# Scaling the first two blocks of x before their transposes, with the front's matmuls in a fixed order

## The chip, the cores and the metric

One core of one Trainium2 chip runs the kernel. The metric is the device time of one execution in microseconds (us), as a median over executions. For this kernel, a difference under 0.5% (3.6 us) is about what a measurement can't tell from no change.

## What is computed

One decoder layer on x of 512 tokens by 2048 features, in float32. What matters here is its start:

```python
c_act = jax.nn.silu(c)
mod = c_act @ w_ada + b_ada
shift, scale, gate = jnp.split(mod, 3, axis=-1)
h = rms_norm(x) * (1.0 + scale) + shift      # rms_norm: x * rsqrt(mean(x*x over features) + EPS)
proj = h @ w_in                              # 2048 -> 4160 columns
# then an RG-LRU branch, an attention branch, an output projection, x + gate * y
```

## The kernel before

Everything after the start works on x transposed: a block k is 128 features (partitions) by 512 tokens, and there are 16 blocks. The input projection `h @ w_in` runs over chunks of 2, 3, 4 and 7 blocks; its first chunk needs blocks 0 and 1 alone. TensorE (PE) works through its instructions in the order that a scheduler fixed when the kernel was built, and so do VectorE (DVE) and ScalarE (ACT). All loads of this part are issued by SyncE (SP) in the written order.

The front, up to the first projection matmul, does this:

- `xsq` loads x token-major in eight pieces `xtok` (128 tokens by 1024 features). ACT squares each and adds up per token. Of the four pieces that hold features 0 to 255, PE transposes two 128x128 tiles each into the PSUM banks `xps[0]` and `xps[1]`. These become blocks 0 and 1 of x.
- `warm(n)` issues n matmuls on a constant tile (`junk`), whose result nobody reads; they keep TensorE busy while it would have nothing to do.
- DVE and ACT turn the sums into the factor `rx` (one number per token, on partitions). Four PE matmuls (`rb_ps`) turn it into a row that is repeated on all partitions, and block 0 is multiplied by it.
- The scale of block 0, `mod[:, 16]`, is made by 16 PE matmuls with one output column each (`m_ps<-ccol,m`), eight from each of two loaded tiles `m0`. All other columns of `mod` are made by DVE: `ttr`, L277, multiplies a row block of the transposed w_ada (`ada`) with silu(c) and sums. `ada(j, parts)` does this for column j in several loads; the parts count in units of 512.
- `make_h(0)` computes `xs` = x block 0 * scale + shift on DVE. `proj_first` multiplies it in full float32 with the first weights (`pp<-xs,wfraw`, 8 matmuls, each of which shows as two rows in the trace), and then block 1, split into a high part `hh[1]` and a low part `hl[1]` (`pp<-h,wfs`, 24 matmuls). `make_h(1)` first needs four more pieces of `ada` (columns 17 and 1). From there on PE goes through weight groups (`pp<-h,whi` and `wlo`) without another kind of matmul for a long time.

Of the kernel before, what the change touches and what calls it, by code (L numbers as in the profile page):

```python
# [12 lines left out]
F32 = mybir.dt.float32  # L13
# [3 lines left out]
AF = mybir.ActivationFunctionType  # L17
ALU = mybir.AluOpType
AX = mybir.AxisListType

P = 128
S = 512
D = 2048
NK = D // P
NT = S // P
# [13 lines left out]
XSTEPS = (36, 40)  # L39
P0 = 8  # L40
SETUP = (0, 2)
WARM = (4, 6, 4, 2, 6)
NACC = 6
GRATE = 1.1
BANKS = dict(u=(0, 1), f=(2,), sc=(4, 5), tp=(6,), op=(6,), tq=(7,), oa=(2, 3, 0, 1, 7, 4, 5, 6))
# [37 lines left out]
def body(ctx, nc, tc, a):  # L83
    V, G, A, PE, DMA = nc.vector, nc.gpsimd, nc.scalar, nc.tensor, nc.sync
    last_tab = [None]

    def act(out, in_, func, **kw):
        return A.activation(out=out, in_=in_, func=func, **kw)  # L88

    def tab(out, in_, func, **kw):  # L90
        if last_tab[0] is None:
            i = act(out, in_, func, **kw)
        else:
            with tc.issue_after(last_tab[0]):
                i = act(out, in_, func, **kw)
        last_tab[0] = i.ins if hasattr(i, "ins") else i
        return i

    def stt(out, in0, scalar, in1, op0, op1, **kw):
        return V.scalar_tensor_tensor(out=out, in0=in0, scalar=scalar, in1=in1, op0=op0, op1=op1, **kw)  # L100
# [3 lines left out]
    def behind():  # L104
        return tc.issue_after(mark[0]) if mark[0] is not None else nullcontext()

    def ins_of(i):
        return i.ins if hasattr(i, "ins") else i

    def ts(o, i, s1, s2, o0, o1=None):  # L110
        if s2 is None:
            return V.tensor_scalar(out=o, in0=i, scalar1=s1, scalar2=None, op0=o0)
        return V.tensor_scalar(out=o, in0=i, scalar1=s1, scalar2=s2, op0=o0, op1=o1)

    def tt(o, x, y, op):
        return V.tensor_tensor(out=o, in0=x, in1=y, op=op)  # L116

    def split(hi, lo, src):
        act(hi, src, AF.Copy)
        return tt(lo, src, hi.bitcast(F32), ALU.subtract)  # L120

    def mm(out, lhsT, rhs, start, stop, **kw):
        return PE.matmul(out=out, lhsT=lhsT, rhs=rhs, start=start, stop=stop, **kw)  # L123
# [6 lines left out]
    def cols(i):  # L130
        return slice(i * P, (i + 1) * P)
# [14 lines left out]
    def run(gen):  # L146
        for _ in gen:
            pass
# [18 lines left out]
    def bank(kind, name):  # L167
        return psp.tile([P, S], F32, tag=f"b{next(cyc[kind])}", name=name)
# [3 lines left out]
    def pjt(n, dt=F32, name=None):  # L172
        return pj.tile([P, S], dt, tag=f"pj{n}", name=name or f"pj{n}")

    def bigt(n, name, dt=F32):
        return big.tile([P, 2, S], dt, tag=f"B{n}", name=name)
# [26 lines left out]
    ident = row[:, R_ID:R_ID + P]  # L203
# [16 lines left out]
    ccol = p1.tile([P, NK], F32, name="ccol")  # L220
# [23 lines left out]
    def warm(n, after=None):  # L244
        with tc.issue_after(ins_of(after)) if after is not None else nullcontext():
            for _ in range(n):
                mm(junk_ps, junk[:, :P], junk, True, True)

    warm(WARM[0])
    cps = [bank("mm", "cb_ps") for _ in range(4)]  # L250
# [9 lines left out]
    xt = {}  # L260
# [14 lines left out]
    def ttr(t, cv, j, first, last):  # L275
        with behind():
            ttr_last[0] = V.tensor_tensor_reduce(  # L277
                out=t, in0=t, in1=cv, op0=ALU.mult, op1=ALU.add, scale=1.0,
                scalar=vec[:, C_BADA + j:C_BADA + j + 1] if first else modh[:, j:j + 1],
                accum_out=(mod if last else modh)[:, j:j + 1])  # L280

    def ada(j, parts=(4,)):
        t = p1.tile([P, 4, S], F32, tag="ada", name="ada", bufs=3)
        n0 = 0
        for w in parts:
            c = slice(n0, n0 + w)
            DMA.dma_start(out=t[:, c], in_=a["ada"][j][:, n0 * S:(n0 + w) * S].rearrange("p (k s) -> p k s", k=w))
            ttr(t[:, c], cb[:, c], j, n0 == 0, n0 + w == 4)
            n0 += w
            yield  # L290
# [79 lines left out]
    def xsq(i, j):  # L370
        t = bigt((2, 3, 8, 9, 10, 11, 12, 13)[2 * i + j], "xtok").rearrange("p k s -> p (k s)")
        DMA.dma_start(out=t, in_=a["xtok"][i][:, j * 1024:(j + 1) * 1024])
        sq = act(sqj, t, AF.Square, accum_out=ss8[:, j * 4 + i:j * 4 + i + 1])
        if j == 0:
            for k in range(KT0):
                PE.transpose(xps[k][:, i * P:(i + 1) * P], t[:, k * P:(k + 1) * P], ident)
        warm(WARM[1], sq)

    hh, hl = {}, {}
    KT0 = CHUNKS[0][1]  # L380
    NG = NF // 4
    wfs = {(k, n): bigt(4 + k * NG + n, "wfs", F32R) for k in range(1, KT0) for n in range(NG)}
# [12 lines left out]
    xps = [bank("mm", "xps") for k in range(KT0)]  # L395
    for n in range(2 * NT):
        xsq(n // 2, n % 2)
# [3 lines left out]
    m0 = [bigt(4 + q, "m0").rearrange("p k s -> p (k s)").rearrange("p (b f) -> p b f", b=8) for q in range(2)]  # L401
    for q in range(2):
        DMA.dma_start(out=m0[q], in_=a["ada0"][:, 8 * q:8 * q + 8])
    run(ada(0, (2, 1, 1)))
    for n in range(NG):
        wf_load(0, n)
    tab(p1.tile([P, 1], F32, name="sqrt0"), ones[:, 0:1], AF.Sqrt)
    for k in range(KT0):
        xt[k] = pjt(34 + k, F32, f"x{k}")
        act(xt[k], xps[k], AF.Copy)  # L410


    vx, yx, tx, rx = (p1.tile([P, NT], F32, name=n) for n in ("vx", "yx", "tx", "rx"))
    tt(vx, ss8[:, 0:4], ss8[:, 4:8], ALU.add)
    ts(vx, vx, 1.0 / D, EPS, ALU.mult, ALU.add)
    warm(WARM[2], V.reciprocal(out=tx, in_=vx))
    tab(yx, tx, AF.Sqrt)
    tt(tx, yx, yx, ALU.mult)
    stt(tx, tx, -0.5, vx, ALU.mult, ALU.mult)
    mark[0] = ins_of(stt(rx, tx, 1.5, yx, ALU.add, ALU.mult))  # L420
    rb_ps = bank("aux", "rb_ps")
    for i in range(NT):
        mm(rb_ps[:, cols(i)], rx[:, i:i + 1].broadcast_to([P, P]), ident, True, True)
    rb = p1.tile([P, S], F32, tag="rb", name="rb")
    tt(xt[0], xt[0], rb_ps, ALU.mult)
    act(rb, rb_ps, AF.Copy)
    m0_ps = bank("mm", "m0_ps")
    for b in range(NK):
        i = mm(m0_ps[:, 0:1], m0[b // 8][:, b % 8], ccol[:, b:b + 1], b == 0, b == NK - 1)
        if b % 8 == 7:  # L430
            warm(WARM[3] if b < NK - 1 else WARM[4], i)
    tt(mod[:, 16:17], m0_ps[:, 0:1], vec[:, 16:17], ALU.add)

    h0 = []
# [1 line left out]
    def make_h(k):  # L436
        if 0 < k < KT0:
            yield from ada(16 + k, (2, 2))
            yield from ada(k, (2, 2))
        x, sc, sh = xt[k], mod[:, 16 + k:17 + k], mod[:, k:k + 1]  # L440
        t = bigt(k, f"h{k}", F32R)
        hh[k], hl[k] = t[:, 0], t[:, 1]
        if k < KT0:
            xs = pjt(30 + k, F32, "xs")
            if k == 0:
                h0.append(xs)
                mark[0] = ins_of(ts(xs, x, sc, sh, ALU.mult, ALU.add))
                split(hh[k], hl[k], xs)
                for k1 in range(1, KT0):
                    with behind():  # L450
                        tt(xt[k1], xt[k1], rb, ALU.mult)
            else:
                act(xs, x, AF.Copy, scale=sc)
                ts(hh[k], xs, sh, None, ALU.add)
                mark[0] = ins_of(stt(hl[k], xs, sh, hh[k].bitcast(F32), ALU.add, ALU.subtract))
        else:
            stt(x, x, sc, rb, ALU.mult, ALU.mult)
            act(hh[k], x, AF.Identity, bias=sh)
            stt(hl[k], x, sh, hh[k].bitcast(F32), ALU.add, ALU.subtract)
        if not k:  # L460
            yield
# [14 lines left out]
    def row_sums(n):  # L476
        while summed[0] < n:
            row_load()
            mark[0] = wlast[0]
            j = rows[summed[0]]  # L480
            ttr(tiles.pop(0), cb, j, True, True)
            summed[0] += 1
            if j < 16:
                run(make_h(j))

    run(make_h(0))
    run(make_h(1))
    for n in range(NG):
        wf_load(1, n)
# [238 lines left out]
    for n, m in enumerate(MORDER[:24]):  # L728
# [23 lines left out]
        for n0, t0 in ((7, 0), (15, 4)):  # L752
            if n0 <= n < n0 + 4:
                t = t0 + n - n0
# [474 lines left out]
```

## Time and profile before

| | us |
|---|---|
| median of 3 timed runs | 726.15 (726.0, 726.15, 728.82) |
| profiled execution, its own time | 725.46 |
| its span, first to last instruction | 723.7 |

The rows below come from the profiled execution; times in them count from the start of its span. A row of the timeline has the start and the duration of one instruction, or of several of a kind that follow each other, with their number (x16). In brackets stand the idle time of the engine before it and what ended that. A matmul's duration is modelled and runs past the start of the next, so that the distance between starts tells what it costs. PEld is TensorE's weight load, which goes on beside the matmul before it.

### The profile page before, as it was taken

How to read it: one execution, taken by the hardware profiler on the slowest of the kernel's cores; microseconds unless marked ns; L12 is line 12 of the kernel's file. 1: busy time of each engine (PE TensorE's matmuls, PEld its weight loads, DVE VectorE, ACT ScalarE, POOL GpSimd, SP SyncE). 2: the span in 40 equal slices, each digit the busy share in tenths (PEclk: the TensorE clock that was granted, in tenths of full speed). 3: DMA queues.
4: the chain of work that ended last, by engine and by line, in shares of the span. 5: the costliest groups of instructions: out<-in, count | busy, mean ns of one | idle time of the engine just before them, and what ended most of it. 6: DMA issues, size and time to landing. Idle time of an engine off the chain costs nothing.

```text
span 723.7 us, 10053 instructions
## 1 busy us (share of the span) xinstructions
PE 718.7 (99%) x3608; PEld 596.0 (82%) x3608; DVE 525.6 (73%) x945; ACT 354.2 (49%) x729; POOL 29.4 (4%) x34
## 2 busy tenths in 40 slices
PE   9999999999999999999999999999999999999998
PEld 4688888888888888888898898898888887888886
DVE  2867999998998889888755566567686786683232
ACT  7277222222233589884455578587465534222221
POOL 0000000000000000001011011111020100000000
PEclk9999999999999999999999999999999999999999
DMA  8998777877613321232342225213334685974330
GB/s 303 408 401 317 297 275 270 352 262 271 241 36 101 108 89 69 90 102 77 93 140 95 81 77 186 71 47 132 125 124 141 219 290 191 318 264 171 115 95 29
DMA packets 46145, 127.95 MB, mean 177 GB/s; under 512 B 5516, under 2 KB 9484, under 8 KB 42512
## 3 DMA queue, kind: packets, MB, share of 16 engines
q1 hardware_dynamic: 39040, 106.35, 41.3%
q10 hardware_dynamic: 7056, 20.97, 8.3%
q8 instruction: 28, 0.46, 0.3%
q14 instruction: 21, 0.17, 0.1%
HBM read 123.11 MB, written 4.19 MB: 176 GB/s over the span
## 4 chain that ended last, share of the span: by engine, by line
PE 99%; DVE 0%; ACT 0%; issue 0%
PE pp L123 48%; PE oa L123 24%; PE sc L123 4%; PE uwuv L123 3%; PE uwqn L123 3%; PE uwuk L123 3%; PE op L123 2%; PE junk_ps L123 2%; PE uqp L123 2%; PE tp L926 1%; PE pk L123 1%; PE tq L826 1%; PE pi L123 1%; PE pr L123 1%; PE tqe L881 0%; PE m_ps L123 0%
## 5 line engine op out<-in xcount | busy, mean ns | idle before, releaser
L123 PE MATMUL pp<-h,whi 128*128 128x512 f32 x992 | 241.1, 390 | 0.0
L88 ACT ACTIVATE whi<-wraw 128x512 fp32r<-128x512 f32 (+4 forms) x172 | 127.0, 741 | 227.7 <-PE pp L123 98.9
L123 PEld LDWEIGHTS pp<-h,whi 128*128 128x128 f32 x992 | 185.1, 188 | 38.3 <-issue 0.4
L116 DVE TENSOR_TENSOR wlo<-wraw,whi 128x512 fp32r<-128x512 f32 (+4 forms) x172 | 141.4, 824 | 72.0 <-ACT whi L88 33.9
L123 PE MATMUL pp<-h,wlo 128*128 128x512 f32 x496 | 126.7, 390 | 0.0
L123 PEld LDWEIGHTS pp<-h,wlo 128*128 128x128 f32 x496 | 92.9, 188 | 19.2
L123 PE MATMUL oa<-yh,whi 128*128 128x512 f32 (+1 forms) x260 | 100.9, 393 | 0.1
L123 PE MATMUL oa<-yl,whi 128*128 128x512 f32 (+1 forms) x260 | 101.0, 389 | 0.0
L116 DVE TENSOR_TENSOR pj<-pp,pj 128x512 f32<-128x512 f32 x96 | 65.0, 689 | 16.6 <-PE pp L123 15.9
L123 PE MATMUL oa<-yh,wlo 128*128 128x512 f32 (+1 forms) x260 | 71.2, 390 | 0.0
L277 DVE CUSTOM_DVE_ANT_0 ada<-ada,cb,vec 128x2048 f32<-128x2048 f32 (+1 forms) x31 | 69.6, 2247 | 1.5 <-DMA ada<-in_ada 1.5
L123 PEld LDWEIGHTS oa<-yl,whi 128*128 128x128 f32 x260 | 49.0, 188 | 9.3 <-DVE yl L116 0.2
L123 PEld LDWEIGHTS oa<-yh,whi 128*128 128x128 f32 x260 | 48.9, 188 | 9.4 <-ACT yh L88 0.3
L123 PEld LDWEIGHTS oa<-yh,wlo 128*128 128x128 f32 x260 | 48.0, 188 | 9.5
L123 PE MATMUL sc<-kT,qT 128*128 128x128 f32 (+3 forms) x96 | 22.5, 331 | 0.0
L918 DVE TENSOR_REDUCE nm<-sc 128x1 f32<-128x128 f32 (+3 forms) x32 | 15.5, 487 | 8.0 <-PE sc L123 7.9
L229 POOL TENSOR_TENSOR hs<-hs,mhalf 128x8 f32<-128x8 f32 x12 | 21.2, 1768 | 1.0
L88 ACT ACTIVATE pr<-sc,nm 128x128 f32<-128x128 f32 (+3 forms) x32 | 16.7, 522 | 9.1 <-DVE nm L918 9.0
L123 PE MATMUL uwuv<-whi,kvt 128*128 128x256 f32 x80 | 20.8, 284 | 0.0
L123 PE MATMUL uwqn<-whi,kvt 128*128 128x256 f32 x80 | 20.7, 286 | 0.0
L277 DVE CUSTOM_DVE_ANT_0 ada<-ada,cbo,modh 128x1024 f32<-128x1024 f32 x16 | 20.5, 1281 | 0.0
L277 DVE CUSTOM_DVE_ANT_0 ada<-ada,cbo,vec 128x1024 f32<-128x1024 f32 x16 | 20.5, 1280 | 0.0
(234 smaller groups left out, 995.8 us busy)
## 6 DMA issues: line engine op xcount, KB each, us to landing
ada<-in_ada SPq DMA_DIRECT2D x28, 1024.0 KB, 7.0
ada<-in_ada ACTq DMA_DIRECT2D x32, 512.0 KB, 5.1
wraw<-in_wout SPq DMA_DIRECT2D x59, 256.0 KB, 3.6
wraw<-in_win SPq DMA_DIRECT2D x22, 512.0 KB, 6.2
wraw<-in_win SPq DMA_DIRECT2D x24, 448.0 KB, 3.2
wraw<-in_win SPq DMA_DIRECT2D x16, 384.0 KB, 5.6
xtok<-in_xtok SPq DMA_DIRECT2D x8, 512.0 KB, 6.6
xo<-in_x SPq DMA_DIRECT2D x16, 256.0 KB, 5.0
```

Source lines behind the costliest of these rows:

```text
L88: return A.activation(out=out, in_=in_, func=func, **kw)
L116: return V.tensor_tensor(out=o, in0=x, in1=y, op=op)
L123: return PE.matmul(out=out, lhsT=lhsT, rhs=rhs, start=start, stop=stop, **kw)
L229: G.tensor_tensor(out=out, in0=out, in1=mhalf[:, :n], op=ALU.pow)
L277: ttr_last[0] = V.tensor_tensor_reduce(out=t, in0=t, in1=cv, op0=ALU.mult, op1=ALU.add, scale=1.0, scalar=vec[:, C_BADA + j:C_BADA + j + 1 ...
L826: PE.transpose(tp[:, d * 256 + i2 * P:d * 256 + (i2 + 1) * P], kt[u][:, q * P:(q + 1) * P], ident)
L918: V.tensor_reduce(out=nm, in_=sp[:, :n], axis=AX.X, op=ALU.max, negate=True)
L926: PE.transpose(tp[:, j * P:(j + 1) * P], pr[:, j * P:(j + 1) * P], ident)
```

## The change

The four head pieces of `xtok` (256 features each) are multiplied by `rx` in place, two on DVE and two on ACT, while still token-major. Then they are transposed, so that the blocks in PSUM are already normalized. Block 0 stays in PSUM and `xs` reads it there; block 1 is copied by ACT. The matmuls of the front get a fixed order: eight `m_ps`, four `rb_ps`, two warm ones, eight transposes, eight `m_ps`, three warm ones. `ada(0)` comes in two parts instead of three. The warm matmuls go from 4 + 48 + 4 + 2 + 6 = 64 to 4 + 42 + 2 + 3 = 51.

```diff
-WARM = (4, 6, 4, 2, 6)
+WARM = (4, 6, 2, 3)
...
         if j == 0:
-            for k in range(KT0):
-                PE.transpose(xps[k][:, i * P:(i + 1) * P], t[:, k * P:(k + 1) * P], ident)
-        warm(WARM[1], sq)
+            xhead.append(t[:, :KT0 * P])
+        if 2 * i + j < 2 * NT - 1:
+            warm(WARM[1], sq)
...
-    run(ada(0, (2, 1, 1)))
+    run(ada(0, (2, 2)))
...
-    for k in range(KT0):
-        xt[k] = pjt(34 + k, F32, f"x{k}")
-        act(xt[k], xps[k], AF.Copy)
...
-    warm(WARM[2], V.reciprocal(out=tx, in_=vx))
+    V.reciprocal(out=tx, in_=vx)
...
+    m0_ps = bank("mm", "m0_ps")
+    for i in range(NT):
+        if i % 2:
+            ts(xhead[i], xhead[i], rx[:, i:i + 1], None, ALU.mult)
+        else:
+            act(xhead[i], xhead[i], AF.Copy, scale=rx[:, i:i + 1])
+    for b in range(NK // 2):
+        i = mm(m0_ps[:, 0:1], m0[0][:, b], ccol[:, b:b + 1], b == 0, False)
     rb_ps = bank("aux", "rb_ps")
-    for i in range(NT):
-        mm(rb_ps[:, cols(i)], rx[:, i:i + 1].broadcast_to([P, P]), ident, True, True)
+    with tc.issue_after(ins_of(i)):
+        for i in range(NT):
+            t = mm(rb_ps[:, cols(i)], rx[:, i:i + 1].broadcast_to([P, P]), ident, True, True)
+    warm(WARM[2], t)
+    with tc.issue_after(ins_of(t)):
+        for i in range(NT):
+            for k in range(KT0):
+                t = PE.transpose(xps[k][:, cols(i)], xhead[i][:, cols(k)], ident)
+    with tc.issue_after(ins_of(t)):
+        for b in range(NK // 2):
+            i = mm(m0_ps[:, 0:1], m0[1][:, b], ccol[:, NK // 2 + b:NK // 2 + b + 1], False, b == NK // 2 - 1)
+    xt[0] = xps[0]
+    for k in range(1, KT0):
+        xt[k] = pjt(34 + k, F32, f"x{k}")
+        act(xt[k], xps[k], AF.Copy)
+    warm(WARM[3], i)
     rb = p1.tile([P, S], F32, tag="rb", name="rb")
-    tt(xt[0], xt[0], rb_ps, ALU.mult)
     act(rb, rb_ps, AF.Copy)
-    m0_ps = bank("mm", "m0_ps")
-    for b in range(NK):
-        i = mm(m0_ps[:, 0:1], m0[b // 8][:, b % 8], ccol[:, b:b + 1], b == 0, b == NK - 1)
-        if b % 8 == 7:
-            warm(WARM[3] if b < NK - 1 else WARM[4], i)
...
                 split(hh[k], hl[k], xs)
-                for k1 in range(1, KT0):
-                    with behind():
-                        tt(xt[k1], xt[k1], rb, ALU.mult)
```

On TensorE, the part between the factor and the scale of block 0 stood like this before (`m_ps` is the scale of block 0, `rb_ps` the repeated factor; the second warm pair is left out):

```order
L123 MATMUL m_ps<-ccol,m_230 128x1 x7
L123 MATMUL rb_ps<-row,rx 128x128 x4
L123 MATMUL m_ps<-ccol,m_230 128x1
L123 LDWEIGHTS junk
L123 MATMUL junk_ps<-junk 128x512
...
L123 MATMUL m_ps<-ccol,m_231 128x1 x8
```

With the change, the same part of TensorE's order is this:

```order
L123 MATMUL m_ps<-ccol,m_216 128x1 x8
L123 MATMUL rb_ps<-row,rx 128x128 x4
L123 LDWEIGHTS junk
L123 MATMUL junk_ps<-junk 128x512
...
L435 MATMUL xps<-row,xtok 128x128 x8
L123 MATMUL m_ps<-ccol,m_217 128x1 x8
```

The eight transposes (`xps`), which stood among the warm matmuls ahead of this part, now stand between the two halves of `m_ps`. Ahead of this part, 23 warm matmuls follow directly behind the `cb_ps` matmuls.

On VectorE, from the first piece of `ada(0)` to `xs` of block 0, the difference is this (ISA is the multiply-and-sum of `ttr` and its read-out):

```order
 L277 ISA ada,modh<-ada,cb,vec 128x1024
 L277 ISA modh 128x1
-L277 ISA ada,modh<-ada,cb,modh 128x512
-L277 ISA modh 128x1
-L116 TENSOR_TENSOR x_245<-x_245,rb_ps 128x512
-L277 ISA ada,mod<-ada,cb,modh 128x512
+L277 ISA ada,mod<-ada,cb,modh 128x1024
 L277 ISA mod 128x1
 L116 TENSOR_TENSOR mod<-m_ps,vec 128x1
-L113 TENSOR_SCALAR xs<-x_245,mod 128x512
-L116 TENSOR_TENSOR x_247<-x_247,rb 128x512
+L113 TENSOR_SCALAR xs<-xps,mod 128x512
```

Both products with the repeated factor are gone, two half pieces of `ada(0)` have become one, and `xs` reads PSUM. The two products on head pieces of `xtok` stand ahead of the first row.

## Rows read from the trace of the kernel before

**Rows 1.** From the profile's page: busy time of each engine, and the share of the span by engine in the chain of work that ended last.

```profile
PE 718.7 (99%) x3608; PEld 596.0 (82%) x3608; DVE 525.6 (73%) x945; ACT 354.2 (49%) x729; POOL 29.4 (4%) x34
...
PE 99%; DVE 0%; ACT 0%; issue 0%
```

**Rows 2.** Timeline of TensorE's matmuls, from the end of `cb_ps` to the first weight group.

```profile
10.28 1.07 PE L123 MATMUL cb_ps<-c4l,sel 4*128 4x512 f32 x4
...
15.01 2.97 PE L123 MATMUL junk_ps<-junk 128*128 128x512 bf16 x13
17.82 0.38 PE L376 MATMUL xps<-row,xtok 128*128 128x128 f32 x2
18.04 1.46 PE L123 MATMUL junk_ps<-junk 128*128 128x512 bf16 x6
19.33 1.62 PE L123 MATMUL m_ps<-ccol,m 128*128 128x1 f32 x14
20.81 1.14 PE L123 MATMUL rb_ps<-row,rx 128*128 128x128 f32 x8
21.79 0.28 PE L123 MATMUL m_ps<-ccol,m 128*128 128x1 f32 x2
21.93 0.59 PE L123 MATMUL junk_ps<-junk 128*128 128x512 bf16 x2
22.36 1.84 PE L123 MATMUL m_ps<-ccol,m 128*128 128x1 f32 x16
24.06 1.46 PE L123 MATMUL junk_ps<-junk 128*128 128x512 bf16 x6
25.35 7.03 PE L123 MATMUL pp<-xs,wfraw 128*128 128x512 f32 x16
31.87 6.00 PE L123 MATMUL pp<-h,wfs 128*128 128x512 f32 x24
37.70 1.07 PE L123 MATMUL pp<-h,whi 128*128 128x512 f32 x4
```

**Rows 3.** Timeline of VectorE, from its copy of `cb` to the high part of block 1.

```profile
10.69 1.29 DVE L258 COPY cb<-cb_ps 128x512 f32<-128x512 f32 x2 [4.72 <-PE cb_ps L123]
...
18.59 0.16 DVE L100 SCALAR_TENSOR_TENSOR rx<-tx,yx 128x4 f32<-128x4 f32 x1
20.02 1.28 DVE L277 CUSTOM_DVE_ANT_0 ada<-ada,cb,vec 128x1024 f32<-128x1024 f32 x1 [1.26 <-DMA ada<-in_ada]
...
22.06 0.69 DVE L116 TENSOR_TENSOR x<-x,rb_ps 128x512 f32<-128x512 f32 x1
...
24.24 0.16 DVE L116 TENSOR_TENSOR mod<-m_ps,vec 128x1 f32<-128x1 f32 x1 [0.82 <-PE m_ps L123]
24.43 0.55 DVE L113 TENSOR_SCALAR xs<-x,mod 128x512 f32<-128x512 f32 x1
24.89 0.69 DVE L116 TENSOR_TENSOR x<-x,rb 128x512 f32<-128x512 f32 x1
25.50 1.28 DVE L277 CUSTOM_DVE_ANT_0 ada<-ada,cb,vec 128x1024 f32<-128x1024 f32 x1
...
29.84 1.28 DVE L277 CUSTOM_DVE_ANT_0 ada<-ada,cb,modh 128x1024 f32<-128x1024 f32 x1
...
31.24 0.49 DVE L112 TENSOR_SCALAR h<-xs,mod 128x512 fp32r<-128x512 f32 x1
31.76 0.75 DVE L100 SCALAR_TENSOR_TENSOR h<-xs,mod,h 128x512 fp32r<-128x512 f32 x1
```

**Rows 4.** Timeline of ScalarE: the first product with a factor per partition, and the high parts of block 1's weights.

```profile
28.63 0.72 ACT L88 ACTIVATE xs<-x,mod 128x512 f32<-128x512 f32 x1 [2.98 <-DVE mod L277]
29.95 1.31 ACT L88 ACTIVATE wfs<-wfraw 128x512 fp32r<-128x512 f32 x2 [0.60 <-DMA wfraw<-in_winf]
```

**Rows 5.** Answers by tile. First the matmuls on the first weights (number of rows; duration in ns, shortest/median/longest; first and last start). Then loads, each with its issue and, in the line below, the time to its landing: the first `m0` tile, the third piece of `ada(0)`, and the four pieces of `ada` for columns 17 and 1.

```profile
L123 PE MATMUL pp<-xs,wfraw x16: 592/592/592, 25.4 to 31.8; 128*128 128x512 f32 x16
...
L403 SPq DMA_DIRECT2D m<-in_ada x1: 327/327/327, 7.6 to 7.6; - x1
...
DMA to landing us min/median/max: 9.8/9.8/9.8
...
L287 SPq DMA_DIRECT2D ada<-in_ada x1: 328/328/328, 13.4 to 13.4; - x1
...
DMA to landing us min/median/max: 7.9/7.9/7.9
...
L287 SPq DMA_DIRECT2D ada<-in_ada x4: 327/328/431, 16.4 to 20.0; - x4
...
DMA to landing us min/median/max: 9.0/9.2/9.3
```

**Rows 6.** Stretches of the span: busy time of the engines (with the number of instructions), the granted TensorE clock, the DMA share and GB/s.

```profile
20.00:24.00 4.00, 4.00 (x37) 3.85 (x37) 3.36 (x7) 0.60 (x1) 0.00 (x0) 1.00 1.05 396
24.00:28.00 4.00, 4.00 (x15) 1.95 (x16) 3.73 (x7) 0.63 (x1) 0.00 (x0) 1.00 1.03 404
```

**Rows 7.** The same of the warm matmuls alone, in two stretches (PE busy with its number of instructions, clock, DMA share, GB/s).

```profile
1.60:6.60 5.00, 5.00 (x12) 1.00 0.68 203
12.30:14.70 2.40, 2.40 (x12) 1.00 1.02 414
```

**Rows 8.** Timeline of VectorE at the turn from the first chunk to the second.

```profile
71.51 0.96 DVE L116 TENSOR_TENSOR wlo<-wraw,whi 128x768 fp32r<-128x768 f32 x1 [4.39 <-ACT pj L88]
```

More of the change, by code (lines that the diff above doesn't have):

```diff
@@ L374, in xsq @@
         if j == 0:
-            for k in range(KT0):
-                PE.transpose(xps[k][:, i * P:(i + 1) * P], t[:, k * P:(k + 1) * P], ident)
-        warm(WARM[1], sq)
-    hh, hl = {}, {}
+            xhead.append(t[:, :KT0 * P])
+        if 2 * i + j < 2 * NT - 1:
+            warm(WARM[1], sq)
+    hh, hl, xhead = {}, {}, []
     KT0 = CHUNKS[0][1]
```

## The prediction

> **What bounds the kernel now.** I read the page first. TensorE is busy 99% of the span, and the chain that ended last is TensorE from end to end [rows 1]. So only what lets TensorE start its real work earlier can shorten the run; DVE and ACT time as such is worth nothing. Next I read TensorE's timeline of the front [rows 2], where the reader should look at the distances between starts. From `cb_ps` to 25.35 us there is no gap: warm matmuls, transposes, the sixteen one-column `m_ps` and the four `rb_ps` stand shoulder to shoulder. At 25.35 the first real matmuls begin, and from there on every matmul is needed. The question is therefore when `pp<-xs` can begin, and how much of what it gains is still there when block 1 and the weight groups follow.
>
> Then I read what feeds these two places. The loads ran at 396 to 404 GB/s with a DMA share of 1.03 to 1.05 between 20 and 28 us [rows 6], so landings there are set by the bytes ahead of them, not by when an engine asks. The first `m0` tile was issued at 7.6 and took 9.8 us, so it landed at 17.4 [rows 5]. For block 1 DVE works through four pieces of `ada` from 25.50 on. They were issued from 16.4 to 20.0 and took 9.0 to 9.3 us: the first landed at 25.4, the last at 29.2 [rows 3, 5].
>
> **What the change does, step by step.**
>
> *Ahead of the scale.* The distance of warm matmuls is (17.82 - 15.01) / 13 = 0.216 us [rows 2]. The 23 that now follow `cb_ps` (which ends at about 10.28 + 4 x 0.216 = 11.14) are done at 11.14 + 23 x 0.216 = 16.1. The next instruction in the fixed order is the first half of `m_ps`, and its tile lands at 17.4. Here a wait of 1.3 us appears that was not there before. It costs nothing as against before, where `m_ps` began only at 19.33, but it is the new bound: with a weight load of about 0.2 us and the wake-up, the first `m_ps` matmul starts at about 17.65.
>
> *From there to the scale.* `m_ps` takes 1.70 for 16 rows (24.06 - 22.36), `rb_ps` 0.98 (21.79 - 20.81), two warm ones 0.43 (22.36 - 21.93), a pair of transposes 0.22 (18.04 - 17.82) [rows 2]. The new sequence is 1.70 + 0.98 + 0.43 + 4 x 0.22 + 1.70 = 5.69, which ends at 23.34 instead of 24.06, a gain of 0.72. The inputs are there in time. `rx` is ready at 18.75 [rows 3], before `rb_ps` at 19.35. The four products on head pieces are not in the trace. A 128x512 product took DVE 0.55 with one more operation, and ACT 0.72 with a factor per partition [rows 3, 4]. For half the columns I bound one between 0.28 and 0.72, so a pair beside each other on the two engines ends between 19.3 and 20.2, ahead of the first transpose at 20.76. They are hidden; if the cover were gone, they would cost up to 1.4.
>
> *From the scale to the first real matmul.* Behind `m_ps` came `mod` after 0.18 and `xs` 0.19 later, which took 0.55 and was ready at 24.98 [rows 3]. Yet `pp` began at 25.35, because six warm matmuls were in front of it: 24.06 + 6 x 0.216 = 25.36. Now three end at 23.34 + 0.65 = 23.99 and `xs` decides: 23.34 + 0.18 + 0.19 = 23.71, plus its duration. It now reads PSUM. A copy from PSUM took 0.65 (1.29 for two), while a two-input product took 0.69 with a PSUM input and without [rows 3]. I take 0.60 between 0.55 and 0.65: ready at 24.3, `pp` at 24.4. That is a gain of 0.95 at this point. DVE is free for it: the second piece of `ada(0)` is complete when its last half lands at 13.4 + 7.9 = 21.3, and a 1024-wide sum takes 1.28, so it ends at 22.7, before `mod` at 23.5 [rows 3, 5].
>
> *From the first to the second block.* Most readers would stop here, but the gain must pass block 1. The 16 rows of `pp<-xs` start from 25.4 to 31.8 [rows 5], 6.4 / 15 = 0.427 apart, so that they take 16 x 0.427 = 6.84: before they were through at 32.19, now at 31.24. `hh[1]` was ready at 31.24 + 0.49 = 31.73, just 0.46 ahead of its use [rows 2, 3]. How much earlier does it come? DVE loses the product with `rb` (0.69, at 24.89), so its first sum can start when its piece has landed, at 25.4 instead of 25.50. The chain behind it is unchanged: four sums, the low part of block 0, `hh[1]`. So it comes 0.1 earlier, at 31.63, and with a wake-up of 0.07 `pp<-h` starts at 31.7. TensorE waits about 0.45 there, and of 0.95 only 32.19 - 31.70 = **0.5 us** is left. The same figure results for any start of `pp` up to 24.85. The high weights are ready in time (first half at 30.6, second at 31.26 [rows 4], eight rows later in use), the low part of block 1 at 32.4 against a need at 33.5.
>
> *Behind it.* `pp<-h,whi` began at 37.70, and no wait of TensorE follows. Nothing else becomes late by half a microsecond: at the turn to the second chunk DVE stood idle for 4.39 us until ACT had evacuated a bank [rows 8], so h was ahead by that much. ACT and DVE swap a few neighbours in the first chunk, inside such slack. So the 0.5 should stay to the end.
>
> *The sum.* 725.46 - 0.5 = 724.96 for an execution like the profiled one. The median of the runs is 0.69 above the profiled time, and on that footing the forecast is 726.15 - 0.5 = **725.7 us**.
>
> **A rule weighed.** The trace shows a transpose of 0.27 us duration, but a pair only 0.22 from start to start of what follows [rows 2]: back to back they overlap. The Trainium skill (TensorE: Matmul & The Clock Gate, Part 4, PE-mode transpose) gives about 275 ns for a 128x128 transpose within a kernel. An estimate by that page, eight of them in a row, is 2.2 us, and the sum by it is the rival of transposes below; I go by the starts.
>
> **The rivals.**
>
> 1. *The clock falls.* At the start of the span 12 warm rows filled 5.0 us, later 12 filled 2.4 [rows 7]: twice the time for the same 512 columns, the levels of 1.2 and 2.4 GHz, though the clock column shows 1.00 for both. It rose after some 5 us of matmuls without a gap. In the front of before TensorE was never idle and the clock held. Now there is 1.3 us of idleness, then 5.7 us with two warm matmuls, and 0.4 idle. If the clock falls just ahead of `pp`, and takes those 5 us to return, six rows are done in 5.1 us where twelve were: 2.55 lost, `pp` ends at 31.24 + 2.55 = 33.8, and the run is 1.6 longer than before. If it falls already at 19.4, `rb_ps`, the warm pair and the transposes double too (0.98 + 0.43 + 0.88 = 2.3): 3.9 longer. So 727.7 to 730.0. It decides as soon as the clock is at its lower level for more than some 2 us in `pp`. For it speaks the thin stretch; against it, that `m_ps`, `rb_ps` and two warm ones from 19.33 to 24.06 kept the clock before, with 1.00 in that stretch [rows 6]. The same page and section of the Trainium skill says that the full clock does not engage for transposes, which would make this rival likelier; no row here shows it. Chance 0.18.
> 2. *The transposes cost their duration.* At 0.27 each the eight take 2.18 instead of 0.88: `pp` begins at 25.7 and ends at 32.55, 0.35 later than before, and 726.5 results. Against it stand the pairs of [rows 2], which however never show more than two. Chance 0.10.
> 3. *Block 1 comes earlier too.* If one load fewer lets the `ada` pieces land half a microsecond sooner, the whole 0.95 is kept: 725.2. Against it stands the DMA share of 1.03 [rows 6]: the bytes ahead are the same. Chance 0.10.
>
> **How the numbers follow.** My forecast has 0.62, with a range of its own from 725.2 to 726.0 (0.2 to 0.9 gained). Forecast, transposes and early block 1 hold 0.82 between 725.2 and 726.5. I widen to 724.6 below, since the profiled execution was 0.69 under the median, and to 728.2 above, which takes in the mild end of the falling clock. Faster by over 0.5% would need 3.6 us; no step offers it: 0.02. Slower by over 0.5% is only the upper end of the first rival: 0.05. Within: 0.93.
>
> **What would show it.** Right: TensorE idle from about 16.1 to 17.5, `m_ps` first; `pp<-xs` at about 24.4; a wait of about 0.45 ahead of `pp<-h` with DVE's `h` as its releaser, at about 31.7; the first weight group about 0.5 before 37.70; the rest as before. Wrong: a distance of 0.85 between rows of `pp<-xs` (the clock), transposes over 0.2 apart, `pp<-xs` later than 24.85, or a first weight group that moves by 0.5 while the end does not, which would put the slack somewhere that I have not found.

## The result: slower, because the clock falls in most executions

| | before | changed |
|---|---|---|
| median, us (22 executions each) | 725.98 (725.0 to 729.27) | 729.76 (724.93 to 733.19) |
| ratio | | 1.0049, 95% interval 1.0036 to 1.0063 |
| profiled execution, its span | 723.7 | 723.1 |

The forecast was 725.7 in a range of 724.6 to 728.2. The one profiled execution is 0.6 us *shorter* in its span than that of before, and yet the median is 3.8 us longer. That is about the 0.5% named ahead as hard to tell from no change, but the interval of the ratio leaves no change out, and so does that of the repetition below (1.0044). The times of the executions explain it, each listed with its mean granted clock (the share of TensorE's full clock that it was given, averaged over the span): 20 of the 22 had a clock of 0.988 to 0.997, one 0.998. The shortest, the profiled one, had 1.000. Of the 94 executions of before that were measured beside the experiments, 7 had 0.997 or less. Below, "fell" counts these: a mean of 0.997 is some 4 us at half clock (2 x 0.003 x 727). A second count takes in those with 0.998, which is a shorter fall. No execution that is listed with 0.999 or 1.000, of any kernel here, took more than 726.7 us.

First the profile after, an execution in which the clock held. TensorE's timeline, to be laid beside [rows 2]:

```profile
11.59 5.14 PE L123 MATMUL junk_ps<-junk 128*128 128x512 bf16 x23
17.81 1.92 PE L123 MATMUL m_ps<-ccol,m 128*128 128x1 f32 x16 [1.08 <-DMA m<-in_ada]
19.59 1.14 PE L123 MATMUL rb_ps<-row,rx 128*128 128x128 f32 x8
20.56 0.59 PE L123 MATMUL junk_ps<-junk 128*128 128x512 bf16 x2
20.99 1.04 PE L435 MATMUL xps<-row,xtok 128*128 128x128 f32 x8
21.86 1.84 PE L123 MATMUL m_ps<-ccol,m 128*128 128x1 f32 x16
23.57 0.81 PE L123 MATMUL junk_ps<-junk 128*128 128x512 bf16 x3
24.81 7.13 PE L123 MATMUL pp<-xs,wfraw 128*128 128x512 f32 x16 [0.43 <-DVE xs L113]
31.38 6.04 PE L123 MATMUL pp<-h,wfs 128*128 128x512 f32 x24
37.25 1.07 PE L123 MATMUL pp<-h,whi 128*128 128x512 f32 x4
```

The forecast's picture is there: a wait for the first `m0` tile, the fixed order, the first weight group 0.45 before 37.70. VectorE of the same execution, beside [rows 3], and the four pieces of `ada`, beside [rows 5]:

```profile
23.94 0.81 DVE L113 TENSOR_SCALAR xs<-xps,mod 128x512 f32<-128x512 f32 x1
24.67 1.27 DVE L277 CUSTOM_DVE_ANT_0 ada<-ada,cb,vec 128x1024 f32<-128x1024 f32 x1
...
30.41 0.49 DVE L112 TENSOR_SCALAR h<-xs,mod 128x512 fp32r<-128x512 f32 x1
```

```profile
L287 SPq DMA_DIRECT2D ada<-in_ada x4: 327/328/431, 16.2 to 19.0; - x4
...
DMA to landing us min/median/max: 7.9/9.7/9.8
```

`xs` took 0.81 from PSUM, and `hh[1]` was ready at 30.9, since the pieces were there sooner than in the execution of before.

### The profile page after: what moved, and what is told of

The parts are those of the page before. It is cut to its first block, busy times and chain, and to the rows that moved or that the text cites. A ratio compares the mean times of both kernels' runs of the same rounds, so it can differ in the third digit from the quotient of the medians.

```text
span 723.1 us, 10030 instructions
## 1 busy us (share of the span) xinstructions
PE 716.7 (99%) x3595; PEld 594.5 (82%) x3595; DVE 525.2 (73%) x943; ACT 354.5 (49%) x730; POOL 29.5 (4%) x34
## 4 chain that ended last, share of the span: by engine, by line
PE 97%; DMA 2%; DVE 0%; SPq 0%; issue 0%; ACT 0%
PE pp L123 49%; PE oa L123 24%; PE sc L123 4%; PE uwuv L123 3%; PE uwqn L123 3%; PE uwuk L123 3%; PE op L123 2%; PE uqp L123 2%; DMA m<-in_ada 1%; PE tp L937 1%; PE pk L123 1%; PE tq L837 1%; PE pi L123 1%; PE pr L123 1%; DMA xtok<-in_xtok 1%; PE m_ps L123 0%
## 5 line engine op out<-in xcount | busy, mean ns | idle before, releaser
L929 DVE TENSOR_REDUCE nm<-sc 128x1 f32<-128x128 f32 (+3 forms) x32 | 15.5, 487 | 7.8 <-PE sc L123 7.7
L88 ACT ACTIVATE pr<-sc,nm 128x128 f32<-128x128 f32 (+3 forms) x32 | 16.7, 522 | 9.0 <-DVE nm L929 8.9
```

The costliest lines, as they stand in the source:

```text
L929: V.tensor_reduce(out=nm, in_=sp[:, :n], axis=AX.X, op=ALU.max, negate=True)
```

## The experiments

Two theories stood against each other. **Clock:** the thinner work of TensorE from 16 to 25 us lets the granted clock fall, and the median is made of such executions. **Something else:** long executions are long at full clock, for instance by loads that come later. Within the first, the parts of the change can share the blame: fewer warm matmuls ahead of `m_ps` (23 for 33; the four that before were tied to the reciprocal stood there too), three for six in front of `pp`, and the transposes' new place. A kernel is named below by its warm matmuls: ahead of `m_ps` / in the middle / in front of `pp`; the change is 23/2/3. Each group of four ran on one chip beside the kernel before.

| kernel | median, us | range | fell | 0.998 or less | ratio to before, 95% interval |
|---|---|---|---|---|---|
| *first chip:* before | 725.69 | 724.87 to 729.27 | 2 of 25 | 5 | |
| change again, 23/2/3 | 729.04 | 728.77 to 729.84 | 5 of 5 | 5 | 1.0044 (1.0026 to 1.0061) |
| hole_filled, 29/2/3 | 726.46 | 724.45 to 731.13 | 3 of 12 | 7 | 1.0009 (0.9991 to 1.0027) |
| order_only, 33/2/6 | 725.47 | 725.02 to 728.48 | 0 of 11 | 1 | 0.9997 (0.9983 to 1.0011) |
| warm_only, 23/2/3, old transposes | 729.23 | 726.58 to 731.15 | 8 of 8 | 8 | 1.0048 (1.0030 to 1.0065) |
| *second chip:* before | 725.82 | 725.12 to 730.79 | 2 of 34 | 7 | |
| mid4, 23/2+4/3 | 729.11 | 727.20 to 733.51 | 8 of 12 | 12 | 1.0050 (1.0029 to 1.0071) |
| hole_mid4, 29/2+4/3 | 729.13 | 725.61 to 732.45 | 5 of 12 | 11 | 1.0039 (1.0021 to 1.0057) |
| hole_tr8, 29/2+8 transposes/3 | 730.32 | 727.29 to 731.64 | 9 of 11 | 11 | 1.0055 (1.0040 to 1.0070) |
| spread, 29/2 behind the transposes/5 | 727.17 | 725.22 to 732.79 | 3 of 12 | 8 | 1.0023 (1.0001 to 1.0044) |
| *third chip:* before | 726.01 | 724.84 to 730.64 | 3 of 35 | 10 | |
| order_again, 33/2/6 | 725.57 | 724.63 to 728.68 | 1 of 12 | 2 | 1.0001 (0.9990 to 1.0011) |
| head33, 33/2/3 | 726.53 | 724.79 to 730.98 | 3 of 12 | 5 | 1.0018 (1.0003 to 1.0034) |
| tail6, 23/2/6 | 729.10 | 724.90 to 734.10 | 9 of 12 | 11 | 1.0039 (1.0016 to 1.0061) |
| before_tail4 (before, four in front of pp) | 725.63 | 725.04 to 726.49 | 0 of 11 | 1 | 1.0000 (0.9992 to 1.0009) |

### The change once more: a long execution in the trace

> The changed kernel once more, for executions with a fallen clock and a trace of one. Clock theory: the median is again 729 to 731, with a mean granted clock of 0.990 to 0.998, and a trace of a long execution shows pp<-xs rows 0.85 us apart instead of 0.43; its loss answers to the stretch at the lower level. Rival (something other than the clock is longer, such as loads that come later): a long execution has clock 1.000 and pp<-xs rows 0.43 apart.

This time the profiled execution is a long one, 727.3 us in its span. TensorE's timeline:

```profile
17.53 1.92 PE L123 MATMUL m_ps<-ccol,m 128*128 128x1 f32 x16 [1.14 <-DMA m<-in_ada]
19.30 1.14 PE L123 MATMUL rb_ps<-row,rx 128*128 128x128 f32 x8
20.28 0.89 PE L123 MATMUL junk_ps<-junk 128*128 128x512 bf16 x2
20.96 1.91 PE L435 MATMUL xps<-row,xtok 128*128 128x128 f32 x8
22.66 3.41 PE L123 MATMUL m_ps<-ccol,m 128*128 128x1 f32 x16
26.32 1.06 PE L123 MATMUL junk_ps<-junk 128*128 128x512 bf16 x2 [0.24 <-issue]
27.17 8.86 PE L123 MATMUL pp<-xs,wfraw 128*128 128x512 f32 x16
35.47 4.69 PE L123 MATMUL pp<-h,wfs 128*128 128x512 f32 x18
```

and stretches of it (start and end, length, busy us and number of instructions of PE, PEld, DVE, ACT, POOL, then the granted clock, DMA share, GB/s):

```profile
18.00:20.00 2.00, 2.00 (x19) 2.00 (x20) 1.12 (x6) 0.93 (x3) 0.00 (x0) 1.00 1.03 410
20.00:22.00 2.00, 2.00 (x11) 1.64 (x11) 1.91 (x3) 0.60 (x1) 0.00 (x0) 0.61 1.04 392
22.00:24.00 2.00, 2.00 (x12) 2.00 (x11) 0.66 (x2) 0.60 (x1) 0.00 (x0) 0.50 1.04 409
...
28.00:30.00 2.00, 2.00 (x4) 0.77 (x3) 2.00 (x4) 0.00 (x0) 0.00 (x0) 0.50 1.07 415
30.00:32.00 2.00, 2.00 (x5) 0.80 (x4) 1.96 (x5) 1.78 (x4) 0.00 (x0) 0.83 1.06 430
32.00:34.00 2.00, 2.00 (x6) 0.95 (x5) 1.86 (x5) 0.93 (x1) 0.00 (x0) 1.00 0.99 401
```

The clock is granted in full until about 20.4 (0.61 over 20 to 22), then at half (the 1.2 GHz level) until about 30.7 (0.83 over 30 to 32), and TensorE is hardly idle there: it does one-column matmuls and transposes. Start by start against the profile after, the eight transposes take 1.70 instead of 0.87, from the second half of `m_ps` to the first `pp<-xs` it is 4.51 instead of 2.95, and from there to `pp<-h` 8.30 instead of 6.57. (The trace has two of the three warm ones in front of `pp`, x2, so that the end of `m_ps` can't be read from their start.) These three lose 0.83, 1.56 and 1.73, the two warm ones before the transposes 0.25, and `m_ps` had begun 0.28 earlier; the wait for `xs` disappears behind the delay. `pp<-h` begins 4.09 later, and the spans differ by 4.2 (727.3 and 723.1). Hardly anything, 0.1, is left for loads or for a later stage: the rival falls.

### Which part of the change lets the clock fall

> The changed kernel (transposes between the halves of m_ps) with the warm matmuls of before, 64 in all: 33 ahead of m_ps, 2 in the middle, 6 in front of pp. If the fewer warm matmuls let the clock fall: it holds here, and the time is that of before within 1 us (m_ps about 0.9 later than in the change, pp at about 26, so 726 to 727). If it is the moved transposes, which make the stretch with two warm matmuls longer: the clock still falls in many executions, 728 to 731.

```diff
-WARM = (4, 6, 2, 3)
+WARM = (4, 6, 2, 6)
...
-        if 2 * i + j < 2 * NT - 1:
-            warm(WARM[1], sq)
+        warm(WARM[1], sq)
...
-    V.reciprocal(out=tx, in_=vx)
+    warm(4, V.reciprocal(out=tx, in_=vx))
```

> The kernel before (transposes among the warm matmuls, x multiplied in transposed form) with the change's 51 warm matmuls and its fixed order of m_ps, rb_ps, warm, m_ps. If the fewer warm matmuls alone let the clock fall: 728 to 731. If it takes the transposes in the thin stretch too: clock near 1.000 in most executions, pp at about 24.2 and 725.3 to 725.8.

```diff
 # the kernel before, with
-WARM = (4, 6, 4, 2, 6)
+WARM = (4, 6, 2, 3)
...
-        warm(WARM[1], sq)
+        if 2 * i + j < 2 * NT - 1:
+            warm(WARM[1], sq)
...
-    warm(WARM[2], V.reciprocal(out=tx, in_=vx))
+    V.reciprocal(out=tx, in_=vx)
# and m_ps (8), rb_ps (4), warm(2), m_ps (8), warm(3) in this fixed order
```

They settle from both sides that the number of warm matmuls decides. With the moved transposes and the old number of warm matmuls the clock holds (0 of 11), and the time is that of before. With the transposes where they were and the new number it falls in 8 of 8. The wait and the fall, in warm_only's timeline of TensorE and in its stretches:

```profile
18.23 3.35 PE L123 MATMUL m_ps<-ccol,m 128*128 128x1 f32 x16 [1.91 <-DMA m<-in_ada]
```

```profile
16.00:18.00 2.00, 0.32 (x3) 0.08 (x1) 0.26 (x2) 1.97 (x6) 0.00 (x0) 1.00 1.03 413
18.00:20.00 2.00, 1.77 (x10) 1.80 (x10) 0.91 (x6) 1.05 (x3) 0.00 (x0) 0.61 1.02 397
```

order_only has no wait there, and `pp` begins as late as before:

```profile
18.40 1.84 PE L123 MATMUL m_ps<-ccol,m 128*128 128x1 f32 x16
...
25.38 7.08 PE L123 MATMUL pp<-xs,wfraw 128*128 128x512 f32 x16
```

### Is it the wait ahead of m_ps or the tail?

> The changed kernel with six more warm matmuls ahead of m_ps (29 instead of 23), which fill the wait for the first m0 tile from 16.7 to 17.8 us and delay nothing. If that idle hole is what lets the clock fall: clock 1.000 and about 725.3, 0.6 under before. If it is the thin stretch behind it (m_ps, rb_ps, two warm ones, transposes, m_ps): the clock still falls in many executions and the median is 727 to 730.

```diff
-        if 2 * i + j < 2 * NT - 1:
-            warm(WARM[1], sq)
+        warm(WARM[1], sq)
```

With six more warm matmuls in the wait, 3 of 12 fell, four more had 0.998, and five executions at a clock of 0.999 or 1.000 took 724.45 to 724.92. In the profiled one the wait is gone and `pp` begins as in the change:

```profile
17.84 1.84 PE L123 MATMUL m_ps<-ccol,m 128*128 128x1 f32 x16
...
24.77 7.13 PE L123 MATMUL pp<-xs,wfraw 128*128 128x512 f32 x16 [0.43 <-DVE xs L113]
```

The median, 726.46, lies between the two that were expected. So the wait is a large part of it, but not all. The third group takes the two ends apart on one chip.

> The change's order with the warm matmuls of before (33, 2, 6), once more, beside the two kernels that take back one half of them each. If the number of warm matmuls decides, whatever chip and whenever the first m0 tile lands: clock 0.998 or more nearly everywhere, 725.4 to 726.2, level with before. If the moved transposes share the blame, it falls clearly more often than before does (2 of 34).

> 33 warm matmuls ahead of m_ps, as before, but three in front of pp, as in the change. If the wait for the m0 tile, which lands at 17.2 to 19.3 us in the profiles so far, is where the clock is lost: it holds, 725.3 to 726. If the thin tail (half of m_ps, three warm matmuls, 0.43 us of waiting for xs) is enough to lose it: it falls in a third of the executions or more, from about 27 us on, 727 to 730 there.

> The reverse: 23 ahead, six in front of pp. If the wait ahead is the cause: clock 0.990 to 0.998 in most executions, median 728 to 730. If the tail is: it holds, 725.3 to 726.

```diff
 # order_again is order_only: 33/2/6
 # head33, against it
-WARM = (4, 6, 2, 6)
+WARM = (4, 6, 2, 3)
 # tail6, against the change
-WARM = (4, 6, 2, 3)
+WARM = (4, 6, 2, 6)
```

The full number holds the clock again (1 of 12 fell), which confirms order_only on another chip. Taking away the ten ahead of `m_ps` makes 9 of 12 fall and costs 3.5 us in the median: the wait weighs most. With the three in front of `pp` taken away, 3 of 12 fell and the median is 0.96 longer. That is hardly clear of chance (order_only and order_again together fell in 1 of 23), and head33's profiled execution held its clock, so the count alone doesn't show that the tail has a share; two traces of the next group do. tail6's trace shows the part of the wait, in TensorE's timeline and its stretches:

```profile
10.38 5.14 PE L123 MATMUL junk_ps<-junk 128*128 128x512 bf16 x22
19.03 3.55 PE L123 MATMUL m_ps<-ccol,m 128*128 128x1 f32 x16 [3.50 <-DMA m<-in_ada]
22.43 2.05 PE L123 MATMUL rb_ps<-row,rx 128*128 128x128 f32 x8
```

```profile
16.00:18.00 2.00, 0.00 (x0) 0.00 (x0) 0.18 (x1) 1.92 (x5) 0.00 (x0) 1.00 1.05 426
18.00:20.00 2.00, 0.97 (x5) 1.00 (x5) 0.89 (x6) 0.98 (x4) 0.00 (x0) 0.66 1.02 408
20.00:22.00 2.00, 2.00 (x11) 2.00 (x11) 1.24 (x4) 0.91 (x2) 0.00 (x0) 0.50 1.03 394
```

The clock fell at about 18.6 (0.66 over 18 to 20), while TensorE still waited. The wait is 3.5 us, not 1.1, from both its ends: the warm matmuls were through at 15.5, 1.2 earlier than in the profile after, and the `m0` tile, issued at 8.3, took 10.6 us and landed 1.2 later:

```profile
L403 SPq DMA_DIRECT2D m<-in_ada x1: 328/328/328, 8.3 to 8.3; - x1
...
DMA to landing us min/median/max: 10.6/10.6/10.6
```

Over the fourteen profiles of this case the tile landed from 17.2 (hole_filled) to 19.3 us (spread). The 33 warm matmuls bridge it up to 19.3 in the profile of before, where the transposes stand among them, and up to 18.2 to 18.5 in the three profiles of 33 with the transposes moved (head33 still waits 0.25). The 23 of the change end at 16.4 and 16.7 in the change's two profiles and at 15.5 in tail6's (start of `m_ps` less the wait), and leave 1.1 to 3.5.

### Filling the middle, and transposes as filling

> The changed kernel with four more warm matmuls between the transposes and the second half of m_ps (0.86 us on TensorE's path); the idle hole ahead of m_ps stays. If the hole is enough to let the clock fall, it still falls in half of the executions or more, 728 to 731 there. If only the thin stretch behind it counts, the clock holds, pp begins at about 25.6 and the time is about 725.7.

> Both: six warm matmuls in the hole and four in the middle. If hole and thin stretch together are the cause, the clock holds in nearly all executions: pp at about 25.6, 725.6 to 726.0, level with before, so that the gain of the change is just the price of keeping the clock. If something else lets it fall, clocks of 0.993 to 0.998 remain in half of the executions.

> As the kernel with hole and middle filled, but with eight transposes of a constant tile (result unread) in the place of the four warm matmuls: about the same time on TensorE, 0.87 us. If a transpose keeps the clock as a matmul does: as the other, clock 1.000 nearly everywhere, 725.6 to 726.0. If transposes do not keep it: the clock falls at least as often as with the hole alone filled (seven of twelve below 0.9985), median 727 or more.

```diff
 # mid4: four warm matmuls behind the transposes; hole_mid4: these, and 29 ahead
+    warm(4, t)
     with tc.issue_after(ins_of(t)):
         for b in range(NK // 2):
             i = mm(m0_ps[:, 0:1], m0[1][:, b], ...
 # hole_tr8, 29 ahead: in their place
+    with tc.issue_after(ins_of(t)):
+        for _ in range(8):
+            t = PE.transpose(junk_ps[:, 0:P], ident, ident)
```

Filling the middle did not help: mid4 fell in 8 of 12, and every one of its executions had a clock of 0.998 or less. hole_mid4 missed its expectation of 725.6 to 726.0: one of its twelve reached 725.61, and the median is 729.13. Its trace shows two falls in one execution, one behind `m_ps` and a second at the start of `pp`, at the wait of 0.43 behind the three warm matmuls:

```profile
21.00:22.00 1.00, 1.00 (x5) 0.45 (x4) 1.00 (x2) 0.60 (x1) 0.00 (x0) 0.50 1.10 410
...
25.00:26.00 1.00, 1.00 (x13) 1.00 (x11) 0.00 (x0) 0.00 (x0) 0.00 (x0) 1.00 1.03 401
...
28.00:29.00 1.00, 1.00 (x2) 0.48 (x3) 1.00 (x3) 0.40 (x1) 0.00 (x0) 0.50 1.06 410
```

hole_tr8's trace has two as well, the second from about 28.5 on, behind the same three and the same wait. So the clock can be lost at the tail too, and after a stretch at full clock. On this chip the profiled `m0` tiles landed at 18.1 to 19.3, later than on the first (17.2 to 18.1), and 29 ahead no longer closed the wait: it was 0.32 in hole_mid4's profile (which names VectorE's `vx` as its end, though the tile had landed only 0.13 before), 1.40 in spread's, 2.25 in hole_tr8's, and 2.08 in mid4's with 23. That mid4 and hole_mid4 did worse than hole_filled on the first chip may come from this alone; it wasn't taken apart. With transposes as filling 9 of 11 fell, with warm matmuls 5 of 12, but the profiled waits differ too (2.25 and 0.32), so whether transposes keep the clock stays open.

### Versions that might beat both

> Hole filled; the two warm matmuls of the middle are moved from ahead of the transposes to behind them, so that work with wide matmuls stands between all thin pieces; five instead of three in front of pp, which fill its wait for xs. Nothing of this is on the path: pp at 24.8. If it matters how the thin pieces are spread: the clock holds more often than with the hole alone filled, and the median is 724.6 to 725.3, under before. If only the amount of warm matmuls counts: as with the hole alone filled, 726 to 727.

```diff
-        if 2 * i + j < 2 * NT - 1:
-            warm(WARM[1], sq)
+        warm(WARM[1], sq)
...
-WARM = (4, 6, 2, 3)
+WARM = (4, 6, 2, 5)
...
-    warm(WARM[2], t)        # ahead of the transposes
+    warm(WARM[2], t)        # behind the transposes
```

> The kernel before with four instead of six warm matmuls in front of pp, as a version that might beat both: there xs was ready 0.3 us before the sixth was through. If nothing hangs on the two: pp at about 25.05, 725.5, or 0.3 under before, with its clock. If the tail needs them: the clock falls in more executions than in before, 726 or more.

```diff
-WARM = (4, 6, 4, 2, 6)
+WARM = (4, 6, 4, 2, 4)
```

spread has the shortest median on the second chip after before, 727.17, with 3 of 12 fallen, which is above both times that were expected of it; its wait was 1.40 in the trace. before_tail4 is level with before within 0.1% either way. In its profiled execution `pp` began at 25.72, not at the 25.05 expected: the clock was at half from 12 to 14 us, among the warm matmuls, `m_ps` began at 19.89 (19.33 before), and the time was 726.12 with a mean of 0.998. So part of the short falls in the second count, of before too, may lie there, where they cost little. Neither beats the kernel before, and order_only and order_again (0.9997 and 1.0001) don't either: their warm matmuls put `pp` back to 25.2 to 25.4, and nothing of the gain is left. Where fewer of them and a kept clock came together, there was a gain: hole_filled's five executions with 0.999 or 1.000 have a median of 724.69, the twenty such of before on that chip 725.50. It is 0.8 us, in five executions of twelve, picked by their clock.

## Why the prediction was wrong

**The step that failed** is the first, *ahead of the scale*: "Here a wait of 1.3 us appears that was not there before. It costs nothing as against before". The arithmetic of the path was right, and the wait was there (1.08 and 1.14 us). But the ten warm matmuls that had filled it were the cover that kept the clock. Taking them away is most of the loss (3.5 us by tail6), taking away three in front of `pp` a smaller part (1.0 by head33, hardly clear of chance). I did name the falling clock as a rival, gave it 0.18, and it happened in 20 of 22 executions.

**Why 0.18 was too low.** I argued that `m_ps`, `rb_ps` and two warm ones had kept the clock from 19.33 to 24.06. That row shows a thin stretch *behind* dense work. In the change a wait stands in front of it, and warm_only shows the fall with the rest of the order nearly as before. I also took the landing at 17.4 from one trace as a constant. It was among the early ones, with 17.2 to 19.3 over the profiles. The end of the 23 warm matmuls moves too, from 15.5 to 16.7, so that the wait is up to three times as long.

**The price of the rival** was 1.6 to 3.9 above before; the median is 3.8 above, at its upper end, which is luck, since the sum was off in its terms. I doubled `rb_ps`, the warm pair and the transposes, and not `m_ps`. In the trace `rb_ps` lost nothing, and the stretch from the second `m_ps` to `pp` 1.56, nearly as much as `pp<-xs` (1.73). I let the clock return after 5 us; in that trace it stayed low for some 10 us and came back 3.5 us after `pp` had begun.

**The gain** of 0.5 was right for an execution whose clock holds: spans of 723.7 and 723.1, the first weight group 0.45 earlier. One pair of executions shows no more than that it is possible, since the twenty of before with a kept clock on the first chip alone differ by 1.6. And the figure is luck, for the path was not as I had it. `pp` began at 24.81 and not at 24.4, since `m_ps` started 0.16 later than worked out and `xs` took 0.81 from PSUM, outside my bounds of 0.55 to 0.65. And block 1 was no bound in that execution: its `ada` pieces had landed earlier, and `pp<-h` followed 6.57 behind the first `pp<-xs`, as close as in [rows 2] (6.52). So 0.54 was gained at `pp` and nearly all of it passed block 1, instead of 0.95 at `pp` and 0.45 lost behind it. In order_again it was the bound, as forecast, with `hh[1]` ready at 32.29 and 7.22 between the two:

```profile
25.21 7.08 PE L123 MATMUL pp<-xs,wfraw 128*128 128x512 f32 x16
32.43 5.72 PE L123 MATMUL pp<-h,wfs 128*128 128x512 f32 x24
```

**The other rivals.** Transposes cost their distance and not their duration: eight took 20.99 to 21.86, 0.87 us, as forecast (0.88). At the lower clock they took 1.70, so that transposes do gain from the full clock where it is granted, against the sentence on transposes that the first rival weighed; whether they keep it stays open. The Trainium skill's 275 ns for one (TensorE: Matmul & The Clock Gate, Part 4, PE-mode transpose) fits the duration of a row and not a series back to back. That the whole gain is kept, since block 1 comes earlier too, is seen in no median. In the profile after it did come earlier, with only 0.54 to keep, and hole_filled's five executions with a kept clock are 0.8 shorter than before's.

## What to carry to other kernels

Matmuls that nobody reads can be load-bearing: before cutting them, ask what TensorE does in the time that they leave, and set their number by the spread of the wait that they bridge, from their own end to the landing, not by one trace. Where a change thins out TensorE's work, list the clock of every execution before reading a profile: the one that was profiled here was the best of 22. And price a fall of the clock by everything that TensorE does until it comes back, one-column matmuls and transposes too.

## What the runs showed of the hardware that I had not expected

- The clock fell while TensorE was at work: in the long execution of the change it had been idle for 1.14 us, and the fall came 2.9 us after that wait had ended, behind one-column matmuls, `rb_ps` and a warm one that stood back to back. The Trainium skill (TensorE: Matmul & The Clock Gate, Part 1) calls the low clock the default, which activity releases; the trace agrees with its two levels (1.00 and 0.50).
- In tail6 the clock fell at about 18.6, still in the wait; in hole_mid4 and hole_tr8 twice in one execution.
- One-column float32 matmuls, whose weight loads filled the stretch (PEld 2.00 of 2.00 us from 20 to 22 in tail6), take nearly twice as long at the lower clock: sixteen rows behind a wait took 3.40 us in tail6 (19.03 to 22.43) and 1.78 in the profile after (17.81 to 19.59).
- VectorE's product with two per-partition numbers took 0.81 us from PSUM and 0.55 from SBUF [rows 3], while the two-input product had shown no difference.
- The load of the first `m0` tile was issued at 7.6 to 9.1 us and took 9.6 to 10.7, so that it landed over a spread of 2.1 us from one profile to another.
